# Two convolution tiles in one PSUM bank, 7 modulation rows moved from layer 2's z to layer 1, taps loaded by GpSimd's queue, and tiles at multiples of 128 bytes

## The chip, the core and the metric

The kernel runs on one core of a Trainium2 chip. The metric is the device time of one execution in microseconds (us); the kernel before took 1924.52 us, the median of three runs from 1924.08 to 1924.67. Engines are named as in the profile: PE is TensorE, PEld its weight loads, DVE VectorE, ACT ScalarE, POOL GpSimd, SP SyncE, which here only issues DMAs.

## What is computed

The reference is a small diffusion transformer in fp32: 256 tokens x, 256 context tokens ctx, width D = 2048, four layers. Layers 0 and 3 mix with a 2-D Fourier transform, layer 1 with windowed attention, layer 2 with a gated depthwise convolution of 31 taps and a layer norm. Cut to what matters here:

```python
for i in range(4):
    shift, scale, gate = split(silu(c) @ ada_w[i] + ada_b[i], 3)
    h = rms_norm(x, norm_g[i]) * (1 + scale) + shift
    o = mix[i](h)
    x = x + gate * o

def conformer_conv_mix(h, w_in, dw_w, dw_b, ln_g, ln_b, w_out):
    a, a_gate, z = split(h @ w_in, 3)
    g = a * sigmoid(a_gate)
    y = depthwise_conv(g, dw_w, taps=31) + dw_b
    y = silu(layer_norm(y, ln_g, ln_b))
    return (y * silu(z)) @ w_out
```

The product silu(c) @ ada_w, 2048 x 6144 in each layer, is what the text calls the modulation. It doesn't depend on x, so it can be computed at any time before the layer that uses it.

## The kernel before, in words

**Weights.** Each matrix product is made of weight pieces of 256 rows by 512 columns (512 KB). `w_piece` loads one by SP's queue into a tile raw (L153, L155), rounds it on ScalarE to whi (L179, two halves) and subtracts that on VectorE, or on GpSimd in layer 2, to wlo (L180). PE then makes three products, hx x whi, hx x wlo and the rest of hx x whi. raw, whi and wlo have three buffers each, so the cast of a piece waits until PE has done the piece three before it. `gemm_T` and `gemm_N` (L193 to L195, L213 to L215) run a projection; `out_proj` (L1114, L1115) runs the output projection: 32 pieces, the first eight of which are two groups of 256 columns side by side and so use all 16 yh tiles, then six groups of four pieces. When a group ends, VectorE adds it to the residual xT (L1126). An out_proj also prepares the next layer: `Deferred` casts xT to hx and `st` gathers the sums of squares ss, which PE adds up over the partitions (pss, L435) within the first chunk of the next layer.

**Modulation rows.** The 2048 x 2048 products of layers 1 to 3 come as 16 rows of 128 x 2048 per part (shift, scale, gate). A row is two loads of 512 KB into the ring aw of four buffers (L328, by SP) and two multiply-adds of 128 x 1024 on VectorE into adacc (L281); in part of layer 2's gated projections PE takes the rows instead. After the 16th row of a part PE and VectorE turn the sum into modc. `ada_v` deals the rows out: `plan(to, steps)` says how far the stream shall be (in quarters of a part, four rows each) after so many weight pieces, and `step()`, called once a piece, takes a row when one is due. The constants T1, T1O, T2, T2Z, T2O and T3S are these targets: by the end of layer 1's input projections, of its out_proj, of layer 2's gated projections, its z, its out_proj, and of the last eight pieces of that out_proj.

**Layer 2.** Eight chunks of gated projections give a pair of channel tiles each (sa, sg); GpSimd multiplies them into one of four padded buffers gp. For each tile ScalarE writes the first tap into a PSUM bank pv (L1244), VectorE adds 30 taps (L1250), ScalarE copies the result to cv (L1252), and VectorE or GpSimd adds it to csum (L1258). The pool has two such banks, so two tiles are in work at a time. The z projection follows (four chunks, 32 pieces; the wlo of the first 23 on GpSimd, of the last nine on VectorE). Beside z runs `ln_part`, the layer norm: the mean from csum (pmean), 16 subtractions (L1270), squares on ScalarE, 16 sums ss (L416), the root, PE's broadcast prs, then for each tile a multiplication (L1279), silu, the product with zt (L1282) and the split into yh (L548), from which the out_proj starts. The taps themselves, conv_dw_w, are loaded by two DMAs dwr of 31 x 1024 into two buffers of the ring aw (L1174), and 16 small transposes pdw on PE (L1201) bring them to dwT.

**What sets the order.** A scheduler lays out each engine's instructions ahead of time; on the chip each engine, and each queue, works off its list strictly in order.

Of the kernel before, what the change touches and what calls it, by code (L numbers as in the profile page):

```python
# [19 lines left out]
P = 128  # L20
# [3 lines left out]
TAPS = 31  # L24
# [4 lines left out]
T0O = 9  # L29
T1 = 14.25  # L30
T1O = 18.25
T2 = 21
T2Z = 21
T2O = 24
T3S = 24.5
SA = 22
# [35 lines left out]
def dit_kernel(ctx: ExitStack, tc: tile.TileContext, x, c, ctxt, c_ctx, norm_g, ada_w, ada_b,  # L72
# [179 lines left out]
    def ada_group(l, s, st):  # L252
# [3 lines left out]
        for kt in range(KT):  # L256
            aw = st.get(l, s, kt)
            if st.pe:
# [208 lines left out]
    class Deferred:  # L467
# [703 lines left out]
    def nxt2():  # L1171
        for i in range(2):
            t = wp.tile([P, D // 2], F32, tag="aw", bufs=AWB, name=nm("dwr"))
            nc.sync.dma_start(t[:TAPS, :], conv_dw_w[0, :, i * 1024:(i + 1) * 1024])  # L1174
            dwr.append(t)
        return Deferred(2)
# [40 lines left out]
    for cg in range(8):  # L1217
# [20 lines left out]
        for ci in range(2):  # L1238
            kt = 2 * cg + ci
            gt = gp[kt % 4]  # L1240
            nc.gpsimd.tensor_mul(gt[:, PAD:PAD + 256], sa[:, 256 * ci:256 * ci + 256], sg[:, 256 * ci:256 * ci + 256])
            pv = psD.tile([P, 512], F32, tag="cv", bufs=2, name=nm("pv"))
            if T0A:
                nc.scalar.activation(pv[:, :256], gt[:, 0:256], AF.Identity, bias=colT[:, kt:kt + 1],  # L1244
                                     scale=dwT[:, kt, 0:1])
            else:
                nc.vector.tensor_scalar(pv[:, :256], gt[:, 0:256], dwT[:, kt, 0:1], colT[:, kt:kt + 1],
                                    op0=ALU.mult, op1=ALU.add)
            for t in range(1, TAPS):
                nc.vector.scalar_tensor_tensor(pv[:, :256], gt[:, t:t + 256], dwT[:, kt, t:t + 1], pv[:, :256],  # L1250
                                               op0=ALU.mult, op1=ALU.add)
            nc.scalar.copy(cv[kt][:], pv[:, :256])  # L1252
            if kt == 0:
                nc.vector.tensor_copy(csum[:], pv[:, :256])
            elif CSP > kt:
                nc.gpsimd.tensor_add(csum[:], cv[kt][:], csum[:])
            else:
                nc.vector.tensor_add(csum[:], pv[:, :256], csum[:])  # L1258

# [199 lines left out]
```

## Time and profile before

| what | value |
|---|---|
| runs | 1924.08, 1924.52, 1924.67 us |
| the profiled execution's own time | 1923.44 us |
| its span in the profile | 1921.4 us |
| PE, DVE, ACT, POOL busy | 97%, 76%, 47%, 12% |
| DMA | 433.64 MB, mean 226 GB/s |
| layer 1: input projections and attention, z, out_proj | 729 to 967, to 1093, to 1194.4 us |
| layer 2: gated projections and convolution, z, out_proj | to 1395, to 1494.7, to 1599 us |
| layer 3: z and u, out_proj and the end | to 1811, to 1921 us |

The profile is one execution's trace. The stages overlap at their borders by a piece or so; the borders above are those of PE. Busy times count the union of an engine's instructions; an instruction's row gives its start, duration, engine, line, operation, and in brackets how long the engine had been idle before it and what released it.

### The profile page before, as it was taken

To read this page: it belongs to the slowest core of one execution; us is meant where nothing else is said; L and a number is where in the kernel's file an instruction comes from. 1 tells how busy PE (TensorE), PEld (TensorE's weight loads), DVE (VectorE), ACT (ScalarE), POOL (GpSimd) and SP (SyncE) were. 2 spreads that over 40 slices of the span, in tenths; PEclk is the share of its full clock that TensorE was granted. 3 is DMA by queue.
4 is the path that set the end of the run, shared out by engine and by line. 5 is a ranking of instruction groups with operands and counts; after the bars stand their busy time and mean duration, and the time that the engine had idled before them with its cause. 6 is when DMAs were issued, how large, how long until landed. Compare 5 with 4: busy or idle time off the path is not lost.

```text
span 1921.4 us, 30258 instructions
## 1 busy us (share of the span) xinstructions
PE 1859.0 (97%) x11143; PEld 1497.9 (78%) x11143; DVE 1452.4 (76%) x2774; ACT 911.0 (47%) x1685; POOL 224.5 (12%) x124
## 2 busy tenths in 40 slices
PE   6999999999999999999999989999999899999997
PEld 5566657777776687866689978999999788889886
DVE  4899954556653458987898678688898999997675
ACT  6333342233322225455556545644455657656553
POOL 0000000000000000000000000788893000000000
PEclk9999999999999999999999999999999999999999
DMA  8888867666778754741568677577766697785553
GB/s 262 282 292 298 302 241 262 201 233 214 240 240 266 272 192 145 245 161 56 187 197 258 206 246 250 187 247 247 256 211 196 213 308 238 244 284 177 165 175 132
DMA packets 247173, 433.64 MB, mean 226 GB/s; under 512 B 16212, under 2 KB 135732, under 8 KB 247026
## 3 DMA queue, kind: packets, MB, share of 16 engines
q1 hardware_dynamic: 245728, 430.25, 68.3%
q8 instruction: 87, 1.43, 0.3%
q10 hardware_dynamic: 1298, 1.48, 0.3%
q14 instruction: 60, 0.49, 0.1%
HBM read 429.56 MB, written 2.10 MB: 225 GB/s over the span
## 4 chain that ended last, share of the span: by engine, by line
PE 78%; DVE 8%; DMA 7%; ACT 3%; issue 2%; POOL 2%; SPq 0%; ACTq 0%; DVEq 0%; POOLq 0%
PE acco L1114 7%; PE accz L193 5%; PE accz L194 5%; PE accz L195 5%; PE accu L213 4%; PE accu L214 4%; PE accu L215 4%; PE acco L1115 3%; DVE wlo L180 3%; PE pa L268 3%; PE acco L193 3%; PE acco L194 3%; PE acco L195 3%; PE accg L193 3%; PE accg L195 3%; PE accg L194 3%
## 5 line engine op out<-in xcount | busy, mean ns | idle before, releaser
L179 ACT CAST whi<-raw 128x512 fp32r<-128x512 f32 (+1 forms) x765 | 540.9, 761 | 664.0 <-PE accu L215 121.3
L180 DVE TENSOR_TENSOR wlo<-raw,whi 128x512 fp32r<-128x512 f32 x682 | 497.3, 778 | 214.7 <-ACT whi L179 209.4
L281 DVE SCALAR_TENSOR_TENSOR adacc<-aw,csil,adacc 128x1024 f32<-128x1024 f32 x188 | 242.7, 1297 | 74.8 <-DMA aw<-in_ada_w_dram 74.7
L1114 PE MATMUL acco<-yh,whi 128*128 128x512 f32 x768 | 276.1, 403 | 9.5 <-ACT whi L179 4.8
L195 PE MATMUL accz<-hx,wlo 128*128 128x256 f32 (+1 forms) x768 | 220.0, 287 | 6.8 <-DVE wlo L180 5.6
L1115 PE MATMUL acco<-yh,wlo 128*128 128x256 f32 x768 | 217.2, 285 | 2.8 <-DVE wlo L180 2.8
L193 PE MATMUL accz<-hx,whi 128*128 128x256 f32 (+1 forms) x768 | 218.0, 284 | 0.0
L194 PE MATMUL accz<-hx,whi 128*128 128x256 f32 x768 | 217.9, 284 | 0.0
L1250 DVE SCALAR_TENSOR_TENSOR pv<-gp,dwT,pv 128x256 f32<-128x256 f32 x480 | 193.0, 485 | 18.9 <-ACT pv L1244 18.3
L180 POOL TENSOR_TENSOR wlo<-raw,whi 128x1024 fp32r<-128x1024 f32 x83 | 201.7, 2441 | 40.3 <-ACT whi L179 37.6
L1114 PEld LDWEIGHTS acco<-yh,whi 128*128 128x128 f32 x768 | 146.1, 191 | 46.6 <-ACT whi L179 5.4
L195 PEld LDWEIGHTS accz<-hx,wlo 128*128 128x128 f32 x768 | 146.7, 191 | 10.3 <-DVE wlo L180 7.3
L1115 PEld LDWEIGHTS acco<-yh,wlo 128*128 128x128 f32 x768 | 146.9, 192 | 7.0 <-DVE wlo L180 5.7
L194 PEld LDWEIGHTS accz<-hx,whi 128*128 128x128 f32 x768 | 146.6, 191 | 1.2 <-issue 0.8
L193 PEld LDWEIGHTS accz<-hx,whi 128*128 128x128 f32 x768 | 146.9, 191 | 0.6 <-ACT whi L179 0.2
L193 PE MATMUL accg<-hx,whi 128*128 128x256 f32 (+1 forms) x512 | 144.9, 284 | 0.3 <-ACT hx L455 0.3
L195 PE MATMUL accg<-hx,wlo 128*128 128x256 f32 (+1 forms) x512 | 143.9, 282 | 0.0
L194 PE MATMUL accg<-hx,whi 128*128 128x256 f32 x512 | 143.3, 280 | 0.0
L1193 POOL MEMSET gp<- 128x286 f32 x4 | 1.2, 338 | 1193.3 <-PE acco L1115 1193.3
L193 PE MATMUL acco<-yh,whi 128*128 128x512 f32 (+1 forms) x272 | 105.9, 390 | 0.0
L193 PEld LDWEIGHTS accg<-hx,whi 128*128 128x128 f32 x512 | 96.2, 188 | 10.8 <-issue 10.3
L194 PE MATMUL acco<-yl,whi 128*128 128x512 f32 (+1 forms) x272 | 103.6, 381 | 0.0
(283 smaller groups left out, 3713.2 us busy)
## 6 DMA issues: line engine op xcount, KB each, us to landing
aw<-in_ada_w_dram SPq DMA_DIRECT2D x376, 512.0 KB, 5.3
raw<-in_four_w_in_dram SPq DMA_DIRECT2D x126, 512.0 KB, 4.9
raw<-in_attn_w_in_dram SPq DMA_DIRECT2D x72, 512.0 KB, 4.0
raw<-in_conv_w_in_dram SPq DMA_DIRECT2D x128, 256.0 KB, 3.4
raw<-in_four_w_out_dram SPq DMA_DIRECT2D x32, 512.0 KB, 5.8
raw<-in_attn_w_out_dram SPq DMA_DIRECT2D x64, 256.0 KB, 4.7
raw<-in_conv_w_in_dram SPq DMA_DIRECT2D x32, 512.0 KB, 4.3
raw<-in_conv_w_out_dram SPq DMA_DIRECT2D x64, 256.0 KB, 4.2
```

The lines of the kernel that those rows point to most:

```text
L179: nc.scalar.copy(hv[:, c], iv[:, c])
L180: eng.tensor_sub(lv[:, c], iv[:, c], hv[:, c].bitcast(F32))
L193: mm(o, a, hh, start=st, stop=False, skip_group_check=True)
L194: mm(o[:, :narrow] if narrow else o, a, hl, start=False, stop=False, skip_group_check=True)
L195: mm(o, b, hh, start=False, stop=kt + k == span[1] - 1, skip_group_check=True)
L213: mm(acc[:], hh, whi[:, k, :], start=st, stop=False)
L214: mm(acc[:], hh, wlo[:, k, :], start=False, stop=False)
L215: mm(acc[:], hl, whi[:, k, :], start=False, stop=kt + k == KT - 1)
L281: ins = nc.vector.scalar_tensor_tensor(acc[:, cs], aw[i][:], cc, acc[:, cs], op0=ALU.mult, op1=ALU.add)
L1114: mm(o[:], whi[:, k, cs], rhs(kt), start=kt == 0, stop=False, skip_group_check=True)
L1115: mm(o[:, :256], wlo[:, k, cs], rhs(kt)[:, :256], start=False, stop=kt == KT - 1, skip_group_check=True)
L1250: nc.vector.scalar_tensor_tensor(pv[:, :256], gt[:, t:t + 256], dwT[:, kt, t:t + 1], pv[:, :256], op0=ALU.mult, op1=ALU.add)
```

## The change

1. **Taps.** The two dwr loads are issued by GpSimd's queue, not SP's.
2. **Bank.** The two tiles of a chunk take the two halves of one PSUM bank, where each had a bank of its own and used half of it. The pool still has two banks.
3. **Rows.** The targets move: 57 rows by the end of layer 1's input projections become 62, 73 by the end of its out_proj become 80, so seven more in layer 1. In layer 2's gated projections PE takes 11 rows in both (73 to 84, 80 to 91). In z none is due. By the end of layer 2's out_proj it is row 96 in both, so 12 rows become 5 there; the two rows planned for its last eight pieces go to layer 3. Layer 3 now takes 16 rows over 46 pieces from its second chunk on, where it took 14 over 60 from its start.
4. **Addresses.** The small tiles sel, cpad and col move or shrink. By the allocator, raw, whi and wlo then begin at 0 and not at 64 modulo 128 bytes, and the buffers of aw at 64 and not at 96.

```diff
-T1 = 14.25
-T1O = 18.25
-T2 = 21
-T2Z = 21
+T1 = 15.5
+T1O = 20
+T2 = 22.75
+T2Z = 22.75
 T2O = 24
-T3S = 24.5
+T3S = 24
...
-            t = wp.tile([P, 40], F32, tag="cpad", name=nm("sh"))
-            self.sh, self.col = t[:, 0:2 * KT].rearrange("p (k r) -> p k r", r=2), t[:, 32:36]
+            t = wp.tile([P, 32], F32, tag="cpad", name=nm("sh"))
+            self.sh = t[:].rearrange("p (k r) -> p k r", r=2)
...
+            if i == 0:
+                self.col = wp.tile([P, 4], F32, tag="rcol", bufs=2, name=nm("col"))
             col = self.col[:, i:i + 1]
...
-            nc.sync.dma_start(t[:TAPS, :], conv_dw_w[0, :, i * 1024:(i + 1) * 1024])
+            nc.gpsimd.dma_start(t[:TAPS, :], conv_dw_w[0, :, i * 1024:(i + 1) * 1024])
...
-            pv = psD.tile([P, 512], F32, tag="cv", bufs=2, name=nm("pv"))
+            if ci == 0:
+                pvb = psD.tile([P, 512], F32, tag="cv", bufs=2, name=nm("pv"))
+            pv = pvb[:, 256 * ci:256 * ci + 256]
...
-    ada_v.plan(28, 60)
...
+        if cg == 1:
+            ada_v.behind = built[0]
+            ada_v.plan(28, 46)
```

**Layer 1's out_proj.** In before, the two dwr loads stand in SP's list among the weights of out_proj (the names are the tiles, raw the weights of a piece):

```order
L328 DMA aw_1945_10665<-in_ada_w_dram 128x1024
L153 DMA raw_1888_10315<-in_attn_w_out_dram 128x2x256 x2
L1174 DMA dwr_1953_10706<-in_conv_dw_w_dram 31x1024
L153 DMA raw_1893_10346<-in_attn_w_out_dram 128x2x256 x2
L1174 DMA dwr_1954_10708<-in_conv_dw_w_dram 31x1024
L153 DMA raw_1896_10371<-in_attn_w_out_dram 128x2x256 x2
L153 DMA raw_1904_10415<-in_attn_w_out_dram 128x2x256 x2
L328 DMA aw_1959_10738<-in_ada_w_dram 128x1024
```

Now they stand in GpSimd's list behind the start-up instructions, and wait for the two buffers of aw. PE's transposes, which stood in layer 2's first chunk, come before the matmuls of the 25th piece of out_proj (whi_1971_10758):

```order
L1116 MATMUL acco_1943_10616<-yh1_1835_9961,wlo_1960_10709 128x256
L1115 MATMUL acco_1944_10617<-yh1_1835_9961,whi_1959_10708 128x512
L1116 MATMUL acco_1944_10617<-yh1_1835_9961,wlo_1960_10709 128x256
L1202 MATMUL pdw_11217<-ident_64,dwr_1967_10748 128x31 x8
L1202 MATMUL pdw_11217<-ident_64,dwr_1968_10750 128x31 x6
L1115 MATMUL acco_1965_10746<-yh1_1719_9073,whi_1971_10758 128x512
L1115 MATMUL acco_1966_10747<-yh1_1719_9073,whi_1971_10758 128x512
L1202 MATMUL pdw_11217<-ident_64,dwr_1968_10750 128x31 x2
L1116 MATMUL acco_1965_10746<-yh1_1719_9073,wlo_1972_10759 128x256
L1116 MATMUL acco_1966_10747<-yh1_1719_9073,wlo_1972_10759 128x256
```

SP's list now has no dwr; its loads of aw_1985_10852 and aw_1986_10854 wait for pdw, and the weights of the last five pieces stand behind them.

**The end of the convolution.** VectorE's list in before, at the last tile's last taps (pv_2284_13833); wlo_2379 and wlo_2382 are the 25th and 26th of z's 32 pieces:

```order
L180 TENSOR_TENSOR wlo_2379_14733<-raw_2377_14730,whi_2378_14732 128x512
L1250 SCALAR_TENSOR_TENSOR pv_2284_13833<-gp3_11035,dwT_11057,pv_2284_13833 128x256
L180 TENSOR_TENSOR wlo_2379_14733<-raw_2377_14730,whi_2378_14732 128x512
L1250 SCALAR_TENSOR_TENSOR pv_2284_13833<-gp3_11035,dwT_11057,pv_2284_13833 128x256
L180 TENSOR_TENSOR wlo_2382_14775<-raw_2380_14772,whi_2381_14774 128x512
L1258 TENSOR_TENSOR csum_11056<-pv_2284_13833,csum_11056 128x256
L180 TENSOR_TENSOR wlo_2382_14775<-raw_2380_14772,whi_2381_14774 128x512
L281 SCALAR_TENSOR_TENSOR adacc_2416_15089<-aw_2432_15200,csil_78,adacc_2416_15089 128x1024
L1270 TENSOR_TENSOR cv0_11040<-cv0_11040,pmean_14251 128x256
L1270 TENSOR_TENSOR cv1_11041<-cv1_11041,pmean_14251 128x256
```

The same place now (the last tile is pv_2291_13831); wlo_2404_14977 and wlo_2407_15009 are z's last two pieces, wlo_2415_15069 is out_proj's first:

```order
L176 TENSOR_TENSOR wlo_2404_14977<-raw_2402_14974,whi_2403_14976 128x512
L1253 SCALAR_TENSOR_TENSOR pv_2291_13831<-gp3_11089,dwT_11111,pv_2291_13831 128x256
L176 TENSOR_TENSOR wlo_2404_14977<-raw_2402_14974,whi_2403_14976 128x512
L1253 SCALAR_TENSOR_TENSOR pv_2291_13831<-gp3_11089,dwT_11111,pv_2291_13831 128x256 x2
L176 TENSOR_TENSOR wlo_2407_15009<-raw_2405_15006,whi_2406_15008 128x512
L1253 SCALAR_TENSOR_TENSOR pv_2291_13831<-gp3_11089,dwT_11111,pv_2291_13831 128x256
L176 TENSOR_TENSOR wlo_2407_15009<-raw_2405_15006,whi_2406_15008 128x512
L1261 TENSOR_TENSOR csum_11110<-pv_2291_13831,csum_11110 128x256
L176 TENSOR_TENSOR wlo_2415_15069<-raw_2413_15065,whi_2414_15068 128x512 x2
L1273 TENSOR_TENSOR cv0_11094<-cv0_11094,pmean_14283 128x256
```

csum, and with it the layer norm, has moved behind the casts of z's last pieces.

**Layer 3's start.** PE's list in before, where the sums of squares are added up (pss); whi_2594_16205 is the third weight piece of layer 3:

```order
L195 MATMUL accz_2586_16138<-hx_2537_15853,wlo_2592_16174 128x258
L193 MATMUL accz_2583_16135<-hx_2541_15882,whi_2594_16205 128x258
L194 MATMUL accz_2583_16135<-hx_2541_15882,whi_2594_16205 128x256
L195 MATMUL accz_2583_16135<-hx_2541_15882,wlo_2595_16206 128x258
L193 MATMUL accz_2583_16135<-hx_2542_15886,whi_2594_16205 128x258
L194 MATMUL accz_2583_16135<-hx_2542_15886,whi_2594_16205 128x256
L195 MATMUL accz_2583_16135<-hx_2542_15886,wlo_2595_16206 128x258
L193 MATMUL accz_2584_16136<-hx_2541_15882,whi_2594_16205 128x258
L194 MATMUL accz_2584_16136<-hx_2541_15882,whi_2594_16205 128x256
L435 MATMUL pss_2599_16267<-ones_69,ss_2403_15030 128x1 x2
L195 MATMUL accz_2584_16136<-hx_2541_15882,wlo_2595_16206 128x258
```

and now, where whi_2579_16150 is the second:

```order
L191 MATMUL accz_2574_16115<-hx_2525_15810,wlo_2577_16119 128x258
L189 MATMUL accz_2571_16112<-hx_2529_15839,whi_2579_16150 128x258
L190 MATMUL accz_2571_16112<-hx_2529_15839,whi_2579_16150 128x256
L191 MATMUL accz_2571_16112<-hx_2529_15839,wlo_2580_16151 128x258
L189 MATMUL accz_2571_16112<-hx_2530_15843,whi_2579_16150 128x258
L190 MATMUL accz_2571_16112<-hx_2530_15843,whi_2579_16150 128x256
L191 MATMUL accz_2571_16112<-hx_2530_15843,wlo_2580_16151 128x258
L189 MATMUL accz_2572_16113<-hx_2529_15839,whi_2579_16150 128x258
L190 MATMUL accz_2572_16113<-hx_2529_15839,whi_2579_16150 128x256
L431 MATMUL pss_2587_16244<-ones_69,ss_2410_15062 128x1 x2
L191 MATMUL accz_2572_16113<-hx_2529_15839,wlo_2580_16151 128x258
```

pss stands one piece earlier.

More of the change, by code (lines that the diff above doesn't have):

```diff
@@ L105, in dit_kernel @@
     nc.vector.memset(eps_t[:], EPS)
-    sel = cp.tile([P, 2], F32, name="sel")
-    for o in range(2):
-        nc.vector.tensor_reduce(sel[:, o:o + 1], ident[:, o:o + 97:32], axis=AX.X, op=ALU.add)
     sel8 = cp.tile([P, 8], F32, name="sel8")
@@ L263, in ada_group @@
                 if fp:
-                    cs = wp.tile([P, 40], F32, tag="cpad", name="cpad")[:, :32]
+                    cs = wp.tile([P, 32], F32, tag="cpad", name="cpad")[:]
                     nc.vector.memset(cs, 0.0)
@@ L668, in dit_kernel @@
     nc.gpsimd.memset(csil0[:], 0.0)
+    sel = aw0.tile([P, 2], F32, name="sel")
+    for o in range(2):
+        nc.vector.tensor_reduce(sel[:, o:o + 1], ident[:, o:o + 97:32], axis=AX.X, op=ALU.add)
     psD = pool(l0, "psD0", PSUM)
@@ L1241, in dit_kernel @@
             nc.gpsimd.tensor_mul(gt[:, PAD:PAD + 256], sa[:, 256 * ci:256 * ci + 256], sg[:, 256 * ci:256 * ci + 256])
-            pv = psD.tile([P, 512], F32, tag="cv", bufs=2, name=nm("pv"))
+            if ci == 0:
+                pvb = psD.tile([P, 512], F32, tag="cv", bufs=2, name=nm("pv"))
+            pv = pvb[:, 256 * ci:256 * ci + 256]
             if T0A:
-                nc.scalar.activation(pv[:, :256], gt[:, 0:256], AF.Identity, bias=colT[:, kt:kt + 1],
+                nc.scalar.activation(pv, gt[:, 0:256], AF.Identity, bias=colT[:, kt:kt + 1],
                                      scale=dwT[:, kt, 0:1])
             else:
-                nc.vector.tensor_scalar(pv[:, :256], gt[:, 0:256], dwT[:, kt, 0:1], colT[:, kt:kt + 1],
+                nc.vector.tensor_scalar(pv, gt[:, 0:256], dwT[:, kt, 0:1], colT[:, kt:kt + 1],
                                     op0=ALU.mult, op1=ALU.add)
             for t in range(1, TAPS):
-                nc.vector.scalar_tensor_tensor(pv[:, :256], gt[:, t:t + 256], dwT[:, kt, t:t + 1], pv[:, :256],
+                nc.vector.scalar_tensor_tensor(pv, gt[:, t:t + 256], dwT[:, kt, t:t + 1], pv,
                                                op0=ALU.mult, op1=ALU.add)
-            nc.scalar.copy(cv[kt][:], pv[:, :256])
+            nc.scalar.copy(cv[kt][:], pv)
             if kt == 0:
-                nc.vector.tensor_copy(csum[:], pv[:, :256])
+                nc.vector.tensor_copy(csum[:], pv)
             elif CSP > kt:
@@ L1257, in dit_kernel @@
             else:
-                nc.vector.tensor_add(csum[:], pv[:, :256], csum[:])
+                nc.vector.tensor_add(csum[:], pv, csum[:])
     def ln_part():
```

## The prediction

> **What bounds the kernel now.** The page comes first: TensorE (PE) is busy for nearly the whole span, so the kernel can gain only where PE stands still or runs slowly.
>
> ```profile
> PE 1859.0 (97%) x11143; PEld 1497.9 (78%) x11143; DVE 1452.4 (76%) x2774; ACT 911.0 (47%) x1685; POOL 224.5 (12%) x124
> ```
>
> The second view cuts the span at the stages that the change touches: layer 1's projections and attention, its z, its out_proj, layer 2's gated pair, its z, its out_proj, and layer 3's z and u. The columns are the stretch, its length, the busy time of PE, PEld, DVE, ACT and POOL with the number of instructions, the granted clock, the DMA share and GB/s.
>
> ```profile
> 729.00:967.00 238.00, 234.94 (x1219) 169.55 (x1217) 204.54 (x475) 132.74 (x320) 0.00 (x0) 0.99 0.50 164
> 967.00:1093.00 126.00, 125.97 (x998) 114.08 (x997) 98.46 (x187) 74.37 (x159) 0.00 (x0) 1.00 0.69 218
> 1093.00:1194.40 101.40, 95.53 (x524) 81.17 (x521) 84.88 (x144) 48.93 (x98) 0.00 (x0) 0.97 0.76 250
> 1194.40:1395.00 200.60, 200.05 (x1669) 187.40 (x1668) 164.46 (x407) 97.69 (x137) 164.90 (x89) 1.00 0.72 235
> 1395.00:1494.70 99.70, 95.45 (x782) 94.16 (x782) 91.83 (x208) 56.16 (x101) 58.72 (x29) 0.98 0.65 205
> 1494.70:1599.00 104.30, 96.98 (x529) 80.97 (x528) 96.45 (x177) 61.41 (x125) 0.00 (x0) 0.97 0.77 254
> 1599.00:1811.00 212.00, 203.77 (x1289) 181.72 (x1288) 184.82 (x277) 132.35 (x205) 0.00 (x0) 0.98 0.71 227
> ```
>
> In the third and the three last rows PE idles 5.9, 4.3, 7.3 and 8.2 us, and the clock is under 1.00. Those two belong together, as a finer cut of the time behind each of the four long stalls shows; for comparison, two stretches of full speed stand with them.
>
> ```profile
> 1140.00:1145.00 5.00, 4.89 (x14) 3.87 (x15) 4.91 (x9) 3.51 (x9) 0.00 (x0) 0.50 0.47 151
> 1145.00:1194.00 49.00, 49.00 (x282) 42.60 (x281) 42.64 (x78) 26.35 (x52) 0.00 (x0) 1.00 0.78 254
> 1474.90:1480.00 5.10, 5.10 (x28) 4.94 (x29) 4.67 (x11) 2.50 (x8) 0.00 (x0) 0.67 0.49 133
> 1480.00:1494.70 14.70, 14.70 (x125) 14.65 (x125) 12.99 (x29) 12.46 (x30) 0.00 (x0) 1.00 0.69 240
> 1525.00:1531.00 6.00, 5.98 (x19) 5.13 (x20) 3.36 (x8) 2.18 (x6) 0.00 (x0) 0.50 0.74 241
> 1533.00:1570.00 37.00, 37.00 (x216) 31.87 (x214) 35.01 (x55) 16.67 (x32) 0.00 (x0) 1.00 0.92 306
> 1609.00:1616.00 7.00, 7.00 (x34) 7.00 (x35) 5.28 (x7) 3.75 (x6) 0.00 (x0) 0.53 0.85 263
> ```
>
> After each stall of 3 us and more PE does about half of its work for 5 to 7 us: at 1140, 14 matmuls instead of 5 x 282/49 = 29. So such a stall costs itself and 1.7 (0.33 x 5.1) to 3.3 us (0.47 x 7). From the same rows comes the pace of a weight piece: 24 matmuls in z, 24 x 14.7/125 = 2.82 us; 16 in out_proj, 16 x 37/216 = 2.74 us.
>
> **Term 1: the taps leave SP's queue (layer 1's out_proj).** The queue of SP, whose second column is the time that the issues of a row take:
>
> ```profile
> 1120.00 0.88 SPq L153 DMA_DIRECT2D raw<-in_attn_w_out_dram  x2
> 1124.06 0.33 SPq L1174 DMA_DIRECT2D dwr<-in_conv_dw_w_dram  x1
> 1126.17 4.72 SPq L153 DMA_DIRECT2D raw<-in_attn_w_out_dram  x4
> 1134.21 8.09 SPq L153 DMA_DIRECT2D raw<-in_attn_w_out_dram  x4
> ```
>
> and ScalarE and PE after it:
>
> ```profile
> 1132.24 1.14 ACT L179 CAST whi<-raw 128x512 fp32r<-128x512 f32 x2 [4.26 <-DMA raw<-in_attn_w_out_dram]
> 1139.43 1.14 ACT L179 CAST whi<-raw 128x512 fp32r<-128x512 f32 x2 [6.06 <-DMA raw<-in_attn_w_out_dram]
> ```
>
> ```profile
> 1132.91 0.51 PE L1114 MATMUL acco<-yh,whi 128*128 128x512 f32 x1 [1.16 <-ACT whi L179]
> 1140.11 0.79 PE L1114 MATMUL acco<-yh,whi 128*128 128x512 f32 x1 [3.62 <-ACT whi L179]
> ```
>
> An issue takes 0.44 us before the two dwr DMAs and up to 2 us after them; the weights land late, ACT waits, and PE stands for 1.16 + 3.62 = 4.8 us and then runs at 0.50, which loses 5 - 14 x 49/282 = 2.6 us: 7.4 in all. The new place is the head of GpSimd's queue, where in layer 1 nothing else is wanted, but the copies still take two buffers of the ring aw and so wait until VectorE has used its rows; PE's 16 transposes pdw now stand in out_proj itself, between its 24th and its 25th piece, some four pieces (4 x 2.74 = 11 us) behind that point. SP's next two aw loads wait for pdw, and the weights of the last five pieces stand behind them. No row shows a copy issued by GpSimd: between nothing and the old hold I take that the stall goes, and 1 us for SP's wait. -7.4 + 1 = **-6.4** (0 to -7.4).
>
> The Trainium skill, "DMA: Bandwidth & Descriptors", section "How many engines (k)", gives a copy the largest number up to 16 that divides its slowest dimension (31 rows: one engine), but says that GpSimd's software queue spreads some direct copies over 16. By the first reading the copy is as slow as before and only its place changes; by the second it is done in a few packets. The trace of before has the first kind only, and both readings are priced below.
>
> **Term 2: seven more rows in layer 1.** A row is two of these instructions:
>
> ```profile
> L281 DVE SCALAR_TENSOR_TENSOR adacc<-aw,csil,adacc 128x1024 f32<-128x1024 f32 x188 | 242.7, 1297 | 74.8 <-DMA aw<-in_ada_w_dram 74.7
> ```
>
> 7 x 2 x 1.297 = 18.2 us of VectorE over three stages in which it is free for 33.5, 27.5 and 16.5 us (first three rows of the stages). It is hidden, but for a cast that comes late now and then: **+1** (0 to +4).
>
> **Term 3: layer 2's z and out_proj.** What goes, by the views of waits:
>
> ```profile
> PE accz L195 <- DVE wlo L180: 3.0, 1, 3.0
> PE acco L1114 <- DVE xT L1126: 2.9, 1, 2.9
> PE acco L1114 <- DVE yh L548: 1.6, 1, 1.6
> ```
>
> With no rows among z's casts the first stall goes, and its clock: z shrinks from 99.7 by 3.0 + 1.7 to about 94 or 95. But VectorE's order moves. In before:
>
> ```profile
> 1462.42 0.48 DVE L1250 SCALAR_TENSOR_TENSOR pv<-gp,dwT,pv 128x256 f32<-128x256 f32 x1
> 1464.12 0.43 DVE L1258 TENSOR_TENSOR csum<-pv,csum 128x256 f32<-128x256 f32 x1 [0.17 <-ACT cv L1252]
> 1466.25 1.41 DVE L1270 TENSOR_TENSOR cv<-cv,pmean 128x256 f32<-128x256 f32 x4
> 1489.38 2.41 DVE L1279 TENSOR_TENSOR cv<-cv,prs 128x256 f32<-128x256 f32 x7 [0.66 <-PE prs L391]
> 1493.10 0.76 DVE L548 TENSOR_TENSOR yh<-cv,yh 128x256 fp32r<-128x256 f32 x2
> 1519.39 0.42 DVE L548 TENSOR_TENSOR yh<-cv,yh 128x256 fp32r<-128x256 f32 x1
> ```
>
> the sum over the channels is done 69 us into z, and the layer norm runs beside z's last third. Now the last tile's taps stand between the casts of z's last nine pieces, and csum behind the last. That cast's buffer is freed when PE has done the third piece before it, 29 x 2.82 = 82 us into z; with the cast, csum falls at +86 or +87 and the first subtraction at +90, not +71.3. From there to the first yh it was 26.9 us; about seven of these were casts and rows that now stand elsewhere, less what the squares on ScalarE hold: 22 (20 to 25). The first yh comes at +112, and PE has been idle since +94: a hole of 18 us where 1.6 stood. Behind it the first eight pieces, which use every yh, take 8 x 2.74 = 22 us, 2.6 for the clock and about 1.5 for waits on yh; then perhaps half of the stall on xT, 1.5; then 24 pieces, 65.8, and 2 for small waits, against 74 in before from 1525 to 1599, since no row stands on VectorE there now. 112 + 22 + 4.1 + 1.5 + 67.8 = 207.4 for both stages, against 99.7 + 104.3 = 204.0: **+3.4** (-4 to +11).
>
> The Trainium skill, "PSUM — Partial Sum Buffer", section "PSUM bank collisions raise a hardware error", wants two engines kept apart by bank, not by column, which speaks against two tiles in one bank: ScalarE can set the first tap of the second half only when VectorE has left the first. The new order does just that and interleaves halves of two banks instead; no run here has two engines in one bank, and the rival below prices what the rule could cost.
>
> **Term 4: layer 3.** PE's longest wait there, and VectorE before it:
>
> ```profile
> PE pss L435 <- DVE ss L416: 3.1, 1, 3.1
> ```
>
> ```profile
> 1600.17 1.25 DVE L281 SCALAR_TENSOR_TENSOR adacc<-aw,csil,adacc 128x1024 f32<-128x1024 f32 x1
> 1604.43 1.29 DVE L281 SCALAR_TENSOR_TENSOR adacc<-aw,csil,adacc 128x1024 f32<-128x1024 f32 x1
> 1608.52 0.41 DVE L416 TENSOR_TENSOR ss<-ss,tmp 128x256 f32<-128x256 f32 x1
> ```
>
> The wait and its clock (0.47 x 7 = 3.3) are 6.4 us. No row stands there now, but pss stands a piece (2.82 us) earlier in PE's order, behind the same chain of casts: I leave 2 us of wait, too short for the clock to fall by the rows above. The 16 rows are denser behind it (46 steps for 60): +1. -6.4 + 2 + 1 = **-3.4** (+1 to -6).
>
> The shift of addresses to multiples of 128 bytes gets **0**: hx halves lie both ways in before, and no row separates them (-3 to +1). The handoffs between tiles are off PE's path, since the order holds csum anyway.
>
> **Sum.** -6.4 + 1 + 3.4 - 3.4 = -5.4. The profiled run took 1923.44, so 1918.0 there; the median is 1.1 higher, 1924.52, so **1919.1**.
>
> **Rivals.** (a) The taps come late, and the end is slower. If the software queue also moves 31 rows on one engine, beside weights, a copy takes as in before: issued at 1124.06, starving the weights until the issues of 1134.21 end at 1142.3, 18 us. The cover is 11 us; PE waits 7, loses 2.6 to the clock, and SP's last weights, held behind pdw, cost some 3 more. In place of -6.4 that is +5.2 (12.6 - 7.4): 1930.7. It decides from a copy of 11 us on. For it: the rows of SP; against: GpSimd's queue is empty. (b) The layer norm catches up: with no casts or rows in its way, its 16 chains take 15 us instead of 22, the hole is 11, term 3 is -4: 1911.7. For it: seven multiplications in 2.41 us at 1489.38; against: ScalarE's squares and the wait for prs. (c) The hole is longer, term 3 at +11, since zt and the casts stand before the squares in ScalarE's order: 1926.7. (d) The shared bank turns the taps into one chain. The page has
>
> ```profile
> L1250 DVE SCALAR_TENSOR_TENSOR pv<-gp,dwT,pv 128x256 f32<-128x256 f32 x480 | 193.0, 485 | 18.9 <-ACT pv L1244 18.3
> ```
>
> 480 taps in 193.0 us, 0.402 each with two chains, against 0.485 for one alone: 480 x 0.083 = 40 us more on VectorE. It is free for 36.1 + 7.9 = 44 us in the two stages of the taps, not all of it where the taps could use it, so some 10 of it would show: 1929. The interleaved order speaks against it.
>
> **How the numbers follow.** Sum as worked 0.50 (its own range 1913 to 1925), (a) 0.15, (b) 0.20, (c) 0.10, (d) 0.05. The range 1908 to 1932 takes in the bounds of terms 1 and 3. A measurement tells 0.2%, 3.8 us: faster is under 1920.7, slower over 1928.4. Of the main case 0.30 lies below, 0.16 between, 0.04 above; (b) is faster, (a) slower, (c) half same and half slower, (d) mostly slower, with a little of it same. Faster 0.50, same 0.24 and slower 0.26.
>
> **What would show it.** Right: no clock of 0.50 within layer 1's out_proj, and raw issues of 0.44 us there; csum behind z's last cast, an idle PE of 15 to 20 us before out_proj 2 and half speed behind it, yet a faster rest; a wait on pss of at most 2 us. Wrong: PE waiting for pdw, a hole under 11 us or over 25, or matmuls whose pace itself has changed.

## The result, and the profile after

The changed kernel takes 1935.8 us (median of four runs, 1933.64 to 1940.41) against 1924.6 for the kernel before: a ratio of 1.0058, 95% interval 1.0042 to 1.0074. The change makes the kernel 11 us slower; the forecast was 1919.1, with a range that ended at 1932. The profiled execution has a span of 1931.5 us.

The first view again is the page's line of the engines, and the second the stages, cut at PE's borders in the new trace: layer 1's projections and attention, z and out_proj, layer 2's gated pair, z (up to PE's last product of z), the rest up to layer 3, and layer 3's z and u.

```profile
PE 1858.0 (96%) x11143; PEld 1493.9 (77%) x11143; DVE 1460.5 (76%) x2772; ACT 910.2 (47%) x1683; POOL 229.3 (12%) x126
```

```profile
728.80:968.60 239.80, 234.80 (x1225) 169.12 (x1224) 193.72 (x465) 133.08 (x320) 0.00 (x0) 1.00 0.42 136
968.60:1095.20 126.60, 126.28 (x991) 113.45 (x989) 110.18 (x197) 72.27 (x156) 0.00 (x0) 1.00 0.78 266
1095.20:1201.60 106.40, 100.70 (x557) 81.26 (x554) 99.15 (x156) 49.90 (x100) 1.21 (x2) 1.00 0.91 310
1201.60:1398.20 196.60, 196.60 (x1636) 184.98 (x1635) 163.24 (x398) 98.14 (x138) 163.84 (x89) 1.00 0.72 234
1398.20:1497.50 99.30, 93.94 (x776) 92.78 (x778) 92.82 (x187) 46.56 (x81) 63.43 (x29) 0.98 0.71 232
1497.50:1612.20 114.70, 97.23 (x539) 83.41 (x532) 91.20 (x194) 70.77 (x143) 0.00 (x0) 0.91 0.49 158
1612.20:1819.50 207.30, 199.73 (x1279) 177.38 (x1278) 183.37 (x275) 132.09 (x205) 0.00 (x0) 1.00 0.71 230
```

PE does the same work in both kernels (1858 us against 1859); all of the difference is waiting. Layer 1's out_proj grew from 101.4 to 106.4 us though its clock is now 1.00 throughout; its DMA share went from 0.76 to 0.91. The gated stage fell by 3.8. The stage that holds layer 2's out_proj grew by 10.4, and layer 3's z and u fell by 4.7. The table below has these lengths for every kernel of this study. It is worked out from each trace as the time from the first product of one stage to that of the next; "z 2 and hole" holds the idle time in front of out_proj 2. Runs of one kernel spread by 1 to 13 us, for most kernels by 5 to 10, part of it ahead of layer 1, so that stages tell more than medians do. But a row of the table is one execution, and a stage varies too: the two kernels that differ only in layer 3's plan have the same order of instructions up to there, and out_proj 1 takes 95.2 us in one and 91.9 in the other. The profiled execution can also lie off the median: "same, old rows" was profiled at 1923.9 us against a median of 1917.5, "rows in z 1" at 1921.3 against 1916.1.

| kernel | attention | z 1 | out_proj 1 | gated | z 2 and hole | out_proj 2 | z, u 3 | ratio to before (95%) |
|---|---|---|---|---|---|---|---|---|
| before | 237.4 | 126.4 | 101.4 | 200.5 | 99.7 | 104.4 | 211.8 | 1 |
| changed | 239.7 | 126.7 | 106.2 | 196.7 | 120.6 | 93.3 | 207.8 | 1.0058 (1.0042 to 1.0074) |
| before, shared bank | 238.2 | 126.4 | 101.1 | 202.0 | 129.7 | 93.7 | 206.5 | 1.0073 (1.0055 to 1.0092) |
| before, taps by GpSimd | 237.4 | 126.4 | 95.2 | 200.3 | 99.2 | 104.2 | 211.6 | 0.9953 (0.9936 to 0.9970) |
| changed, two banks | 238.8 | 128.8 | 107.7 | 196.6 | 102.4 | 95.9 | 209.5 | 0.9990 (0.9978 to 1.0001) |
| same, old rows in layers 1, 2 | 237.7 | 126.4 | 94.4 | 200.1 | 104.7 | 100.5 | 215.5 | 0.9968 (0.9956 to 0.9980) |
| changed, thin multiplies | 238.4 | 128.8 | 104.6 | 196.1 | 115.0 | 93.1 | 208.1 | 1.0011 (0.9996 to 1.0026) |
| changed, thin loads | 240.2 | 126.5 | 90.7 | 217.4 | 119.9 | 92.9 | 210.4 | 1.0098 (1.0072 to 1.0124) |
| changed, both thin | 238.0 | 125.6 | 92.7 | 197.8 | 119.3 | 92.3 | 208.6 | 0.9988 (0.9970 to 1.0005) |
| before, addresses | 237.3 | 126.4 | 100.2 | 200.8 | 104.0 | 98.1 | 213.5 | 0.9994 (0.9981 to 1.0007) |
| before, taps, layer 3's plan | 237.1 | 126.4 | 91.9 | 200.7 | 100.1 | 105.8 | 216.3 | 0.9982 (0.9967 to 0.9997) |
| two banks, rows in z 1 | 239.1 | 135.6 | 95.2 | 197.8 | 101.4 | 98.2 | 209.6 | 0.9954 (0.9939 to 0.9968) |
| before, taps, T1 = 17 | 241.1 | 127.1 | 93.9 | 205.7 | 102.1 | 101.7 | 211.5 | 1.0013 (0.9999 to 1.0028) |
| two banks, T1 = 17 | 241.6 | 128.1 | 103.0 | 199.5 | 102.8 | 98.6 | 210.9 | 1.0007 (0.9990 to 1.0024) |

**Layer 1's out_proj.** GpSimd's queue issues the taps, and the view of waits of PE over this stage (line, what it waited for, us in total, times, longest) has little of them:

```profile
1164.56 0.71 POOL L1175 DMA_DIRECT2D dwr<-in_conv_dw_w_dram  x1 [1163.15 <-DMA aw<-in_ada_w_dram]
1166.62 0.50 POOL L1175 DMA_DIRECT2D dwr<-in_conv_dw_w_dram  x1 [1.36 <-DVE adacc L277]
```

```profile
PE acco L1115 <- ACT whi L175: 2.5, 5, 0.8
PE acco L1116 <- DVE wlo L176: 2.5, 5, 1.3
PE pdw L1202 <- DMA dwr<-in_conv_dw_w_dram: 0.5, 1, 0.5
```

No wait here is over 1.3 us, where before had one of 3.6. Yet from 1142 to 1196 all but one of the 14 weight pieces take 3.2 to 5.6 us instead of 2.8. ScalarE, which casts the weights, tells why; its first line of waits in the stage, in the changed kernel and then in before:

```profile
ACT whi L175 <- DMA raw<-in_attn_w_out_dram: 23.1, 13, 3.6
```

```profile
ACT whi L179 <- DMA raw<-in_attn_w_out_dram: 20.4, 8, 6.1
```

and the issues in the last third, with the stretches of 10 us around them:

```profile
1168.74 1.54 SPq L324 DMA_DIRECT2D aw<-in_ada_w_dram  x2
1175.45 1.87 SPq L324 DMA_DIRECT2D aw<-in_ada_w_dram  x2
1177.72 7.07 SPq L149 DMA_DIRECT2D raw<-in_attn_w_out_dram  x6
```

```profile
1135.00:1145.00 10.00, 9.77 (x56) 8.33 (x56) 8.46 (x15) 4.99 (x11) 0.00 (x0) 1.00 1.01 354
1155.00:1165.00 10.00, 8.48 (x44) 6.28 (x44) 9.69 (x16) 4.48 (x10) 0.44 (x1) 1.00 1.05 370
1175.00:1185.00 10.00, 8.17 (x46) 6.51 (x45) 9.55 (x16) 2.47 (x6) 0.00 (x0) 1.00 1.04 373
```

Two long stalls became many short ones: ScalarE waits for weights 13 times instead of 8, the DMA engines are full (share 1.01 to 1.05 at 354 to 373 GB/s), and VectorE is busy for over 95% of the last two stretches. About 5 us of those 14 pieces are other work of PE: the 16 transposes and the small products that end a part of the modulation (L291, L296) stand among them now, three microseconds of which stood in the gated stage before. The trace counts 30 loads of rows in the stage where before had 16.

**Layer 2.** VectorE from the last csum to the first yh, and PE over the same time:

```profile
1490.55 0.42 DVE L1261 TENSOR_TENSOR csum<-pv,csum 128x256 f32<-128x256 f32 x1
1492.30 1.41 DVE L1273 TENSOR_TENSOR cv<-cv,pmean 128x256 f32<-128x256 f32 x4
1508.79 0.42 DVE L412 TENSOR_TENSOR ss<-ss,psq 128x256 f32<-128x256 f32 x1 [0.45 <-ACT psq L408]
1511.89 1.28 DVE L277 SCALAR_TENSOR_TENSOR adacc<-aw,csil,adacc 128x1024 f32<-128x1024 f32 x1 [2.68 <-DMA aw<-in_ada_w_dram]
1513.10 0.16 DVE L382 RECIPROCAL rcol<-rcol 128x2 f32<-128x2 f32 x1
1518.33 0.76 DVE L546 TENSOR_TENSOR yh<-cv,yh 128x256 fp32r<-128x256 f32 x2
```

```profile
1509.27 1.01 PE L431 MATMUL pss<-ones,ss 128*128 128x1 f32 x4 [11.02 <-DVE ss L412]
1513.74 1.22 PE L387 MATMUL prs<-tmp,ones 128*128 128x256 f32 x2 [2.61 <-ACT tmp L385]
1518.80 0.79 PE L1115 MATMUL acco<-yh,whi 128*128 128x512 f32 x1 [3.84 <-DVE yh L546]
```

csum stands at +92 of z and not at +69, and PE idles three times in a row: from the end of z at 1497.3 to 1518.8 it does 21.5 us of nearly nothing. Behind that, out_proj 2 runs without a stall.

Why csum comes so late is seen where ScalarE writes a tile's first tap and copies a finished tile out. In before, the second tile begins 3 us behind the first:

```profile
1225.56 0.58 ACT L1244 ACTIVATE pv<-gp,colT,dwT 128x256 f32<-128x256 f32 x1
1228.84 0.57 ACT L1244 ACTIVATE pv<-gp,colT,dwT 128x256 f32<-128x256 f32 x1 [0.97 <-POOL gp L1241]
```

In the changed kernel the first tile is copied out (L1255) before the second and the third begin together:

```profile
1231.40 0.58 ACT L1247 ACTIVATE pv<-gp,colT,dwT 128x256 f32<-128x256 f32 x1
1253.24 0.36 ACT L1255 COPY cv<-pv 128x256 f32<-128x256 f32 x1
1255.01 1.06 ACT L1247 ACTIVATE pv<-gp,colT,dwT 128x256 f32<-128x256 f32 x2 [1.41 <-POOL gp L1242]
1455.67 0.49 DVE L1253 SCALAR_TENSOR_TENSOR pv<-gp,dwT,pv 128x256 f32<-128x256 f32 x1 [3.05 <-ACT pv L1247]
```

The second tile's input was ready at 1234.64, when GpSimd's second product ended. So the first tile's 30 taps run alone, then the tiles go in pairs, and the last tile is alone again: its 30 taps run from 1455.67 to 1490.04 among casts and rows, where before the last tile had four taps left when the tile beside it was copied out.

**Layer 3.** PE's wait on the sums of squares fell from 3.1 to

```profile
PE pss L431 <- DVE ss L412: 1.2, 1, 1.2
```

and the clock of the stage is 1.00.

### The profile page after: what moved, and what is told of

It reads as the page before. It is cut to its first block, busy times and chain, and to the rows that moved or that the text cites. A ratio compares the mean times of both kernels' runs of the same rounds, so it can differ in the third digit from the quotient of the medians.

```text
span 1931.5 us, 30222 instructions
## 1 busy us (share of the span) xinstructions
PE 1858.0 (96%) x11143; PEld 1493.9 (77%) x11143; DVE 1460.5 (76%) x2772; ACT 910.2 (47%) x1683; POOL 229.3 (12%) x126
## 4 chain that ended last, share of the span: by engine, by line
PE 78%; DVE 9%; DMA 6%; ACT 3%; issue 2%; POOL 1%; SPq 0%; POOLq 0%; ACTq 0%; DVEq 0%
PE acco L1115 7%; PE accz L189 6%; PE accz L190 6%; PE accz L191 6%; PE accu L209 4%; PE accu L210 4%; PE accu L211 4%; PE acco L1116 4%; DVE wlo L176 3%; PE accg L189 3%; PE accg L191 3%; PE accg L190 3%; PE pa L264 3%; DMA aw<-in_ada_w_dram 3%; PE acco L189 3%; PE acco L190 3%
## 5 line engine op out<-in xcount | busy, mean ns | idle before, releaser
L1253 DVE SCALAR_TENSOR_TENSOR pv<-gp,dwT,pv 128x256 f32<-128x256 f32 x480 | 195.5, 481 | 22.5 <-ACT pv L1247 21.4
```

What stands on the lines that cost most here:

```text
L1253: nc.vector.scalar_tensor_tensor(pv, gt[:, t:t + 256], dwT[:, kt, t:t + 1], pv, op0=ALU.mult, op1=ALU.add)
```

## The experiments

The theory after this reading has three parts. The shared bank makes the hole in layer 2 (A); the taps' move cures what it was said to cure (C); and what spoils layer 1's out_proj is the rows, of which VectorE's list has 32 halves there and not 18, because their loads and the weights together are more than the DMA engines move (M). Rivals: the hole comes from the planner or the rows (B), GpSimd's copies disturb the weights (D), VectorE's list is the bound of the out_proj (V).

**Before with the shared bank alone.**

```diff
+            if ci == 0:
+                pvb = psD.tile([P, 512], F32, tag="cv", bufs=2, name=nm("pv"))
+            pv = pvb[:, 256 * ci:256 * ci + 256]
```

> The kernel before with the shared bank alone; the rows, the taps and the addresses stay as they were. VectorE's order then puts the last csum behind the casts of out_proj's second piece, not of z's 26th. Theory A (the shared bank itself makes the hole between layer 2's z and its out_proj): PE stands 20 us or more before that out_proj, and with rows still among z's casts and in the layer norm the kernel is 10 to 18 us slower than before, 1935 to 1943 us; layer 1 stays as in before. Rival B (the hole comes from the moved rows or the planner, not from the bank): within 4 us of before, 1921 to 1929 us.

Measured 1938.5 us. VectorE has csum at 1496.31, 100 us into z, and PE waits for what follows:

```profile
1496.31 0.42 DVE L1260 TENSOR_TENSOR csum<-pv,csum 128x256 f32<-128x256 f32 x1
```

```profile
PE pss L435 <- DVE ss L416: 19.3, 1, 19.3
PE pmean L1266 <- DVE csum L1260: 2.9, 1, 2.9
```

Theory A holds and B falls: layer 1 is unchanged (101.1), z and the hole take 129.7 us for 99.7. Of these 30 us, 10.7 come back in out_proj 2 and 5.3 in layer 3, since the rows that stood there are worked off in the hole.

**Before with the taps on GpSimd's queue alone.**

```diff
-            nc.sync.dma_start(t[:TAPS, :], conv_dw_w[0, :, i * 1024:(i + 1) * 1024])
+            nc.gpsimd.dma_start(t[:TAPS, :], conv_dw_w[0, :, i * 1024:(i + 1) * 1024])
```

> The kernel before with the taps' two loads on GpSimd's queue alone. Theory C (the move cures the stall of layer 1's out_proj as predicted, and what slows that stage in the changed kernel are the seven rows that its order put there): no clock of 0.50 in the stage, the stage falls from 101.4 to about 93 or 94 us, the kernel to 1916 to 1919 us. Rival D (copies of GpSimd's queue slow the weights as much as before, only spread out): the stage stays over 99 us, the kernel at 1922 us or more.

Measured 1915.7 us. The out_proj is one row of the stages:

```profile
1095.40:1190.60 95.20, 93.04 (x524) 79.23 (x521) 85.18 (x144) 49.10 (x98) 1.21 (x2) 1.00 0.83 267
```

It fell by 6.2 us, no clock is low, and every other stage stands as in before within 0.5 us. Theory C holds, though the stage stays a little over the 93 or 94 us expected; D falls. The two other kernels below with the taps moved and the old rows there have 91.9 and 94.4 us. This is the whole of what the change could have gained in layer 1.

**The changed kernel with a bank for each tile.**

```diff
-            if ci == 0:
-                pvb = psD.tile([P, 512], F32, tag="cv", bufs=2, name=nm("pv"))
-            pv = pvb[:, 256 * ci:256 * ci + 256]
+            pvb = psD.tile([P, 512], F32, tag="cv", bufs=2, name=nm("pv"))
+            pv = pvb[:, 0:256]
```

> The changed kernel with a bank for each tile again; all else as changed. VectorE's order has csum behind the cast of z's 27th piece again. Theory A: the hole of 21 us before layer 2's out_proj falls to under 4 us, and the kernel to 1918 to 1924 us, 12 to 18 under the changed one; layer 1's out_proj stays at 106 us. Rival B: the hole stays over 12 us and the kernel over 1930 us.

Measured 1921.6 us, 14.2 under the changed kernel. csum is back at 71 us into z (which starts at 1399.9), and the hole is 2 us:

```profile
1471.09 0.42 DVE L1260 TENSOR_TENSOR csum<-pv,csum 128x256 f32<-128x256 f32 x1 [0.66 <-ACT cv L1254]
```

z, hole and out_proj 2 take 198.3 us against 213.9: the bank costs 15.6 us. Undone or done alone, it decides the hole. Layer 1's out_proj stays slow, as expected (107.7 us for 106.2, with 3.4 us at a clock of 0.5 behind a wait of 1.4):

```profile
1095.60:1203.30 107.70, 101.33 (x557) 82.24 (x554) 99.28 (x156) 49.59 (x99) 1.21 (x2) 0.98 0.92 309
```

**Two banks, and the old rows in layers 1 and 2.**

```diff
-T1 = 15.5
-T1O = 20
-T2 = 22.75
-T2Z = 22.75
+T1 = 14.25
+T1O = 18.25
+T2 = 21
+T2Z = 21
 T2O = 24
-T3S = 24
+T3S = 24.5
```

> As the kernel with two banks, and the targets of layers 1 and 2 as in before, so that 18 half rows, not 32, stand in layer 1's out_proj; layer 3's new plan, the taps on GpSimd's queue and the addresses stay. Theory C (the rows in that out_proj cost 12 to 14 us there): layer 1's out_proj falls from 106 to about 93 us, and some 4 to 6 us come back in layer 2, where transposes, group ends and rows return: 5 to 9 us under the kernel with two banks, about 1912 to 1917 us. Rival D (the copies of GpSimd's queue hold that stage): the stage stays over 100 us, and the kernel within 3 us of the one with two banks.

Measured 1917.5 us, 4.1 under the kernel with two banks, where 5 to 9 were expected. The out_proj falls by 13.3 us to

```profile
1095.10:1189.50 94.40, 92.53 (x525) 79.54 (x522) 85.57 (x146) 48.92 (x98) 1.21 (x2) 1.00 0.83 270
```

so the rows made the stage 13 us longer, and D falls again. What they gave elsewhere is lost: 3.5 in the gated stage, 6.9 in layer 2's z and out_proj, 6.0 in layer 3. These losses are read from an execution 6.4 us slower than the kernel's median, so they may be high.

**Thin multiplies, thin loads, both thin.** Three kernels ask what in a row costs this. They are the changed kernel; in layer 1's out_proj only, a row's multiply-adds, or its loads, or both take 64 of 1024 columns. The edits, where thin is set around that out_proj:

```diff
-                    cs = slice(w * i, w * i + w)
+                    cs = slice(w * i, w * i + (64 if thin[0] and not fd else w))
```

```diff
+                if thin[0]:
+                    t = t[:, 0:64]
-                nc.sync.dma_start(t[:], ada_w[l, kt * P:(kt + 1) * P, c0:c0 + D // 2])
+                nc.sync.dma_start(t[:], ada_w[l, kt * P:(kt + 1) * P, c0:c0 + t.shape[1]])
...
+                    if av.shape[1] == 64:
+                        av = av.unsqueeze(1).to_broadcast([P, 16, 64])
```

> The changed kernel, but in layer 1's out_proj each row's multiply-adds take 64 of their 1024 columns (part of the modulation is left out), while the loads stay whole. Read from the stage's length, 106.3 us in the changed kernel and 95.2 in the kernel before with the taps alone. Theory V (VectorE's list is the bound there: casts stand behind multiply-adds of 1.28 us): the stage falls to 94 to 98 us. Rival M (the loads are the bound: 30 of 512 KB beside the weights): it stays over 103 us. If both count, it lies between, and the next kernel gives the other share.

> The changed kernel, but in layer 1's out_proj each row's two loads bring 64 of their 1024 columns, which the multiply-adds, at full length, read 16 times (the modulation is then another one). Theory V: the stage stays over 103 us. Rival M: it falls to 94 to 98 us.

> The changed kernel, but in layer 1's out_proj both the loads and the multiply-adds of the rows take 64 of 1024 columns (part of the modulation is left out); the same 32 half rows stand there in VectorE's order. It asks where the gated stage of the kernel with thin loads lost 21 us. Theory W (with the loads out of the way VectorE is the next bound, and its backlog of multiply-adds held the casts at the next stage's start): now the out_proj takes 91 to 97 us and the gated stage 196 to 200 us, so both together fall from 302.9 us to about 290 to 296. Rival (thin loads upset the gated stage by themselves, through the order): the gated stage stays over 210 us.

The out_proj in the three, in this order:

```profile
1094.40:1199.00 104.60, 99.04 (x553) 82.31 (x554) 73.40 (x161) 49.35 (x99) 1.20 (x2) 0.98 0.92 314
```

```profile
1097.20:1187.80 90.60, 90.48 (x521) 78.65 (x522) 89.12 (x138) 48.95 (x98) 1.21 (x2) 1.00 0.63 196
```

```profile
1091.30:1184.10 92.80, 92.48 (x541) 80.18 (x538) 73.98 (x161) 49.37 (x99) 1.21 (x2) 1.00 0.66 209
```

With thin multiplies VectorE is busy for 73 us, not 99, and the stage takes 104.6 us all the same: theory V falls. (That kernel's 1925.1 us owe most of their gain to layer 2, where its order has csum a piece earlier.) With thin loads the DMA share falls from 0.91 to 0.63 and the stage to 90.6: M holds. Not all of that fall is the loads': PE's transposes and the small products at the end of a part take 6.0 us of the stage in the changed kernel, 0.8 with thin loads and 2.6 with both thin, as they moved to the next stage. Without them the stage falls by 10.3 and 10.1 us. But the kernel with thin loads is at 1941.9, because the gated stage behind takes 217.4 us for 196.7: waits of 3.4 us for ss, 3.2 for hx and 3.2 for GpSimd's casts stand there. By theory W, PE ran ahead of VectorE, which still had its multiply-adds; but the order also leaves five more half rows to that stage. With both thin the two stages take 92.7 and 197.8 us, 290.5 together against 302.9, as W had it. That order leaves no more half rows to the gated stage than the changed kernel's, though, so the order as the cause of the 217.4 is not excluded. So the loads are the bound of the stage, and with them thin PE is busy for 90.5 of its 90.6 us; that VectorE's multiply-adds would bind next is argued, not shown.

**Rows in z 1 instead.** From here on M was used to place the rows: the kernel with two banks and T1 = 18.5 (for 15.5), and as smaller steps T1 = 17 (for 14.25) in before with the taps moved, and T1 = 17 in the kernel with two banks.

> The changed kernel with two banks, and T1 raised from 15.5 to 18.5, so that the order has 52 half rows beside layer 1's z and 12 in its out_proj, where the kernel with two banks alone has 32 and 32; everything behind layer 1 is as there. Theory M (the loads bound the out_proj: 30 half rows beside its weights are too many): the out_proj falls from 107.7 to about 92 to 95 us; z, which moved 266 GB/s, then moves some 350 and grows from 128 by 2 to 8 us; together 6 to 12 us less, the kernel at 1910 to 1916 us. Rival (a half row costs the same wherever it stands in layer 1): both stages together stay within 3 us, the kernel at 1919 us or more.

> The kernel before with the taps on GpSimd's queue and T1 at 17: the order has 38 half rows beside layer 1's z and 12 in its out_proj, where the kernel with the taps alone has 32 and 18. Theory M: the out_proj falls from 95.2 by 1 to 4 us and z stays within 1 us, so the kernel is at 1911 to 1915 us. Rival (18 half rows are already hidden there): within 1 us of the kernel with the taps alone, 1915.7.

> As the kernel with two banks, T1 at 17: 38 half rows beside layer 1's z and 26 in its out_proj. Theory M: the out_proj lies between the kernels with 12 to 18 and with 32 half rows there, at 99 to 103 us, if its cost grows with each row past what the loads carry; the kernel at 1915 to 1919 us. Rival (a step, not a slope): 106 us or more, or under 97.

The first: 1916.1 us. Its trace has 33, 40 and 12 half rows beside the attention, z 1 and out_proj 1, where the kernel with two banks has 21, 32 and 32: twelve of the 52 that were expected beside z stand beside the attention's last pieces. z 1 and out_proj 1 are

```profile
969.10:1104.70 135.60, 130.70 (x1012) 116.09 (x1010) 121.34 (x215) 70.86 (x162) 0.00 (x0) 1.00 0.77 261
1104.70:1199.90 95.20, 93.29 (x528) 79.45 (x529) 80.38 (x142) 49.55 (x98) 1.21 (x2) 1.00 0.80 261
```

so the out_proj gained 12.5 us and z lost 6.8, together 5.7, a little less than expected. The twelve half rows beside the attention cost next to nothing (239.1 us for 238.8). z did not move the 350 GB/s that were expected but 261 in the mean; from 1070 to 1090, though, its DMA share is 1.04 and 1.00, and PE idles for 4.7 us from 1070 to the end. The other 2 us of its loss are open. The trace of the third has 36 and 26 half rows beside z and the out_proj and gave the slope: 103.0 us, between 92 to 95 (12 to 18 half rows) and 107.7 (32), so 0.8 to 1.1 us for each half row past 18, PE's small products that moved with the rows included. But in time the second and the third missed, 1928.9 and 1925.8 us. Of their out_proj stages the third's, 103.0, came out as expected; the second's, 93.9, is 1.3 us under the kernel with the taps alone, and 2.0 over the kernel of layer 3's plan, which has the taps-alone order there (91.9), so it shows no gain. The attention took 241 to 242 us for 237 to 239, and the gated stage 5.4 and 2.9 more. In the second, PE waits 1.8 us for ss and 1.6 us for aw there; the rest, and the 3 us in the attention, stay open.

**Before with the addresses alone.** The edits of sel, cpad and col as in the change.

> The kernel before with the addresses alone: sel, cpad and col moved or shrunk, raw, whi and wlo at 0 modulo 128 bytes. VectorE's order moves a little with it: csum stands two casts later. Theory 0 (addresses do nothing): a piece of z still takes 2.82 us and one of out_proj 2.74 to 2.83, the multiply-adds 1.28; the kernel within 3 us of before, by the order alone. Rival: transfers or reads get faster, pieces and rows take less time, the kernel is 3 us or more under before.

Measured 1921.4 us, a ratio of 0.9994 whose interval, 0.9981 to 1.0007, holds 1. A piece of z takes 2.83 us, one of out_proj 2.77, a multiply-add 1.277, all as in before; the stages that differ (104.0 and 98.1 in layer 2, 213.5 in layer 3) lie behind the place from which its order is another, with csum two casts later. Addresses do nothing that these runs can tell.

**Before with the taps and layer 3's new plan.**

```diff
-    ada_v.plan(28, 60)
...
+        if cg == 1:
+            ada_v.behind = built[0]
+            ada_v.plan(28, 46)
```

> The kernel before with the taps on GpSimd's queue and layer 3's new plan (rows from its second chunk on, 46 steps), no other part of the change. Theory: the wait on pss (3.7 us in the kernel with the taps alone) falls to 2 us or less and the clock holds, so layer 3's z and u fall from about 212 to 206 to 209 us and the kernel to 1910 to 1914 us. Rival (the denser rows behind give it back): z and u stay at 210 us or more, the kernel within 2 us of 1915.7.

Measured 1921.1 us: the theory falls. Layer 3's z and u take 216.3 us, 4.7 more than with the taps alone, and PE still waits 3.1 us for ss, as in before. VectorE's list shows why: five half rows stand in layer 3's first chunk as before (six), put there by the target T3S, and the rest is denser behind. In the changed kernel none stands there, and the kernel with two banks and the old rows, which has four there, takes 215.5. So the plan alone doesn't bring term 4's gain; it came with a first chunk without rows. No run parts the two things that emptied it, the target T3S and the rows done in layer 1.

## Why the prediction was wrong, step by step

**Term 1, the taps: right in mechanism and size.** Predicted -6.4; with the taps moved alone, the out_proj fell by 6.2 us (by 7.0 and 9.5 in two other kernels with that order). The clock's part of it was real: no 0.50 is left in the stage. Rival (a), the taps landing late, did not come: PE waited 0.5 us for them. The page counts 96 packets for the two copies, and the view of DMAs has them landing 4.5 us after issue:

```profile
q0 software_dynamic: 96, 0.25, 0.0%
```

```profile
dwr<-in_conv_dw_w_dram POOLq DMA_DIRECT2D x2, 124.0 KB, 4.5
```

In the trace the 31 packets of 4096 bytes of a copy, 0.16 to 0.20 us each in the median, overlap, each copy's within 1.5 us, and 17 packets of 4 bytes go with each copy. In before one came behind the other, over 10 us. That is the second reading of the Trainium skill's "DMA: Bandwidth & Descriptors", "How many engines (k)" in the section "Why a DMA increments its semaphore by 16 and not by 1": GpSimd's queue spread this copy of 31 rows over the engines.

**Term 2, the seven rows: the step that failed.** The prediction spread them over three stages "in which it is free for 33.5, 27.5 and 16.5 us" and said +1. Two things were wrong. First the place: VectorE has 33, 20 and 18 half rows beside the attention, z and the out_proj in before, and 21, 32 and 32 in the changed kernel. The attention and z together have 53 in both, since twelve moved from the one to the other, and all 14 new halves are in the out_proj. The targets give the step at which a row is asked for, and the list shows where it ends up; it could have been counted. Second the resource: VectorE's free time was weighed, not the DMA engines', and the kernels with thin loads and thin multiplies show that the loads hold the stage. That row of before had a share of 0.76, lowered by the stall on the taps; without it the stage stands at 0.83, and seven rows of 1 MB take it to 0.91 to 0.92. Against the kernel with the taps alone the out_proj is 11.0 us longer; 3.8 of these are group ends and transposes that left the gated stage, so the rows cost 7.2 net. Between the two kernels with two banks it is 13.3 and 3.5, 9.8 net. No rival of the prediction had this cost, and +7.2 lies outside the bounds 0 to +4.

**Term 3, layer 2: the mechanism right, the size too small, by as much as term 2's.** Predicted +3.4 for z and out_proj 2 together, measured 213.9 against 204.1, +9.8, within the bounds -4 to +11. The hole was read off the order as predicted, 18 us against 21.5. Three sizes were off. z did not shrink to 94: its pieces 11 and 22 take 3.3 and 1.8 us more behind GpSimd's casts, and csum holds PE for 2.2. Nor was z free of rows: eight half rows stand in it, though none is due, while out_proj 2 has none left of its 19. And the 3.3 us are a wait of 2.0, followed by a clock of 0.50 from 1430.9 to 1434.3; the prediction held a wait of 2 us to be too short for that. The way from the first subtraction to the first yh took 26.0 us and not 22, because three half rows still stood in it; the last, waiting for its load at 1511.89, held the reciprocal that stands behind it by about 1.7 us. The rest of out_proj 2 ran better, 93.3 for 95.4.

Of the rivals, (b), a layer norm that catches up, fell. Rival (c), at +11, is near what came in its number only: most of the excess is z's, and the rows in the layer norm, which (c) did not name, account for part of the rest. (d) fell, since the taps interleave: VectorE needs 195.5 us for the 480 taps, against 193.0 in before and the 40 more of the rival. The Trainium skill's "PSUM — Partial Sum Buffer", section "PSUM bank collisions raise a hardware error", asks to keep engines apart by bank. The rows of the trace agree: the second half's first tap at 1255.01 comes behind the copy of the first half at 1253.24. What the shared bank costs here is that wait, by which the tiles go in staggered pairs and the last one ends alone: 15.6 us by the kernel with two banks. Whether the second half waits because it shares the bank or because it shares the tile is not told by these runs.

**Term 4, layer 3: near in size, half right in cause.** Predicted -3.4, measured -4.0; the wait on pss was 1.2 us where 2 was left. The six other kernels that begin layer 3 without rows take 208.1 to 210.9 us there, so the saving is 1 to 4 us and the changed kernel's the largest. The new plan alone makes the stage longer by 4.7.

**Addresses: 0, as predicted.**

The sum: -6.2 for the taps, +7.2 for the rows in place of +1, +9.8 in place of +3.4, -4.0, and what no term had, 2.3 in the attention's stage and 0.9 in the last: +10.0, against 10.1 between the two spans. Two terms were near; the two that were too low are the rows, by 6.2, and layer 2, by 6.4. The 2.3 in the attention are open: the other kernels with the same 21 half rows beside it take 0.6 to 2.8 us more than before. The taps alone (1915.7 us, 0.9953) and the changed kernel with two banks and more rows ahead of the out_proj (1916.1, 0.9954) beat both kernels.

## What to carry to other kernels

Work that is moved "to where the engine is free" has to be costed on its loads as well: here 14 half rows of 512 KB fitted VectorE and did not fit the DMA engines, and the stage had looked freer than it was because a stall had thinned its traffic. Count in the order where moved work really stands, since a planner's target is only the time it is asked for. And when two chains are made to share a guarded resource, look at what stands behind the chain that now ends last: a half-used bank saved cost 15.6 us because the last tile was left alone and one sum slipped from among the first of VectorE's nine casts to behind the last.

## What the hardware did that was not expected

- A stage can be slow without a stall worth a line: in layer 1's out_proj no wait of PE was over 1.3 us, and 14 pieces together lost some 15 us, of which about 5 were other work of PE.
- Taking the loads away brought out_proj to 90.7 us and made the next stage 20.7 us slower; with the multiply-adds thin too, and in another order, the gain stayed (92.7 and 197.8 us).
- The clock falls behind short waits too, and not each time: seven kernels begin layer 3 in the same way and wait 1.1 to 1.3 us on pss; in two of them, "rows in z 1" and "two banks, T1 = 17", the next 3.4 us ran at a clock of 0.50, in the others at 1.00.
- A copy of 31 rows on GpSimd's queue landed in 4.5 us; on SP's queue its packets ran one behind the other for some 10.
